# Merge gates of a hybrid decoder trunk: one 512-column product for both parts of the moving operand, and the halves of its bank added on the way out

## The chip, the cores and the metric

The kernel runs on one core of one Trainium2 chip. The metric is the device time of one execution in microseconds (us). TensorE is called PE, VectorE DVE, ScalarE ACT, GpSimd POOL, SyncE SP.

## The reference, cut to what matters

Two layers are computed for 256 tokens of width 1024, all in float32. In each layer one projection of the normalised tokens gives everything that the token mixers need, the two merge gates among it:

```python
h = rms_norm(x, norm_mix[l])
z = h @ w_in[l]
c_q, c_kv, k_pe, hq, hf, hi, hg, g_a, g_b = jnp.split(z, offsets, axis=-1)
y_a = mla_mixer(c_q, c_kv, k_pe, ...) @ w_proj_a[l]
y_b = hgrn2_mixer(hq, hf, hi, hg, ...) @ w_proj_b[l]
y = jax.nn.sigmoid(g_a) * y_a + jax.nn.sigmoid(g_b) * y_b
x = x + y @ w_out[l]
h = rms_norm(x, norm_ffn[l])
x = x + (jax.nn.silu(h @ w_gate[l]) * (h @ w_up[l])) @ w_down[l]
```

The gates g_a and g_b have 1024 columns each. They are the part of the projection that the change touches; the sigmoid is computed as a Tanh of half the value.

## The kernel before, in words

**Split operands.** PE takes float32 in a reduced form (F32R), so each operand is held as a high part and a low part, and a product a·b is computed as ah·bh + ah·bl + al·bh. A weight chunk of 2048 columns (two tiles of 8 blocks of 128 x 128) is loaded by one transfer into `st`; for each half of 1024 columns ACT casts the high part `wh` (line 115) and DVE subtracts to get the low part `wl` (line 117). There are three buffers for `st` and five for each of `wh` and `wl`; `weights` (line 122) lets the loads run one chunk ahead. The moving operand is `xx`, a tile in which for each k the high and the low part of the tokens lie side by side, 256 columns each.

**Two forms of a tile's product.** `mm3` (line 196) issues three products of 256 columns for each k (lines 206 to 208), all into the same 256 columns of a PSUM bank, so two tiles share one bank of 512 columns. `mmw` (line 210) multiplies the high weights by both parts at once, one product of 512 columns (line 214), and adds the low weights times the high part into the first half of the bank (line 215); the two halves of the bank are still to be added. The feed-forward stage has used `mmw` from the start: its gate and up tiles leave by an ACT copy of the second half (line 738), a DVE addition of the first (line 739) and a multiplication by the row scale `rb` (line 740, the first tile on DVE, the second on POOL). The down projection uses `mmw` too.

**The order of a layer.** `norm_in` makes `xx` and `rb`. Then come the chunks t0 to t2 and one chunk in token order, the latent projections of the attention, t3 to t6, and a hand-written interleaving (lines 679 to 691): before each of the chunks t7 to t16 one step of the generator `rec` (the recurrence) is issued, and before t8, t10, t12 and t14 one step of `at` (the attention). Chunks t9 to t16 hold the merge gates, sixteen tiles in a layer. After that come the projection `proj`, the output product `out`, a second `norm_in`, and the feed-forward stage. Within these lines a scheduler plans the order of each engine's instructions by a modelled timeline, with PSUM's and the buffers' slots in view; on the chip each engine then works through its instructions in that order.

**PSUM.** Four pools of two banks each: `acc`, `prj`, `trp`, `hgp`. A chunk of `tchunk` takes one bank of `acc` for its two tiles. `prj` serves the attention's scores, the last of which are issued before t12.

**A gate chunk's way out before.** `tchunk` (lines 267 to 287) multiplies the whole bank by `rb` on DVE into `gs` (line 286) and takes the Tanh on ACT into `gab` (line 287), which the projection stage uses at line 709.

Of the kernel before, what the change touches and what calls it, by code (L numbers as in the profile page):

```python
# [9 lines left out]
F32 = mybir.dt.float32  # L10
# [3 lines left out]
AF = mybir.ActivationFunctionType  # L14
ALU = mybir.AluOpType
AX = mybir.AxisListType

P = 128
T = 256
TT = T // P  # L20
D = 1024
KD = D // P
# [59 lines left out]
def trunk(ctx: ExitStack, tc: tile.TileContext, x_in, w_in, vec_in, gqk_in, cst_in, msk_in, out):  # L82
    nc = tc.nc
    V, S, G, PE = nc.vector, nc.scalar, nc.gpsimd, nc.tensor
# [5 lines left out]
    wk = ctx.enter_context(tc.tile_pool(name="wk", bufs=2))  # L90
    acc = ctx.enter_context(tc.tile_pool(name="acc", bufs=2, space=bass.MemoryType.PSUM))
    prj = ctx.enter_context(tc.tile_pool(name="prj", bufs=2, space=bass.MemoryType.PSUM))
# [8 lines left out]
    def load(upto):  # L101
        while nxt[0] < min(upto, len(order)):
            l, n, w = order[nxt[0]]
            st = stage.tile([P, WMAX], F32, name="st")
            o = OFFS[n]
            step = w // 2 if nxt[0] == 1 else w
            for c in range(0, w, step):
                nc.sync.dma_start(st[:, c:c + step], w_in[l, :, o + c:o + c + step])
            sub = SUB[w]
            parts = []  # L110
            for c in range(0, w, sub):
                wh = wsp.tile([P, 1088], F32R, name="wh")
                wl = wsp.tile([P, 1088], F32R, name="wl")
                n_ = min(sub, w - c)
                S.copy(wh[:, :n_], st[:, c:c + n_])  # L115
                eng = G if (n, c // sub) in ON_POOL or nxt[0] == 0 else V
                eng.tensor_tensor(wl[:, :n_], st[:, c:c + n_], wh[:, :n_].bitcast(F32), ALU.subtract)  # L117
                parts.append((wh, wl))
            ready[(l, n)] = lambda o, m, parts=parts, sub=sub: tuple(t[:, o % sub:o % sub + m] for t in parts[o // sub])
            nxt[0] += 1  # L120

    def weights(l, n):
        i = order.index((l, n, dict(PLAN)[n]))
        load(i + 2)
        return ready.pop((l, n))
# [57 lines left out]
    def bc(ap, shape):  # L183
        return ap.broadcast_to(shape)
# [11 lines left out]
    def mm3(ps, pairs, late=False):  # L196
        n = len(pairs)
        if late:
            for i, ((ah, al), (bh, bl)) in enumerate(pairs):
                PE.matmul(ps, ah, bh, start=i == 0, stop=False)  # L200
                PE.matmul(ps, ah, bl, start=False, stop=False)
            for i, ((ah, al), (bh, bl)) in enumerate(pairs):
                PE.matmul(ps, al, bh, start=False, stop=i == n - 1)
            return
        for i, ((ah, al), (bh, bl)) in enumerate(pairs):
            PE.matmul(ps, ah, bh, start=i == 0, stop=False)  # L206
            PE.matmul(ps, ah, bl, start=False, stop=False)  # L207
            PE.matmul(ps, al, bh, start=False, stop=i == n - 1)  # L208

    def mmw(ps, items):  # L210

        n = len(items)
        for i, ((ah, al), b) in enumerate(items):
            PE.matmul(ps, ah, b, start=i == 0, stop=False)  # L214
            PE.matmul(ps[:, 0], al, b[:, 0], start=False, stop=i == n - 1)  # L215
# [19 lines left out]
    def norm_in(l, col):  # L235

        xx = lay.tile([P, KD, 2, T], F32R, name="xx")
        xh, xl = xx[:, :, 0], xx[:, :, 1]
        for k in range(KD):
            split(xh[:, k], xl[:, k], xT[:, k], vec[:, l, col + k:col + k + 1])  # L240
        ss = token_stats(xT, KD, both=True)
        ms = wk.tile([P, TT], F32, name="ms")
        V.tensor_scalar(ms, ss, 1.0 / D, EPS, ALU.mult, ALU.add)
        r = lay.tile([P, TT], F32, name="r")
        power(r, ms)
        dg = wk.tile([P, TT, P], F32, tag="gs", name="dg")
        for t in range(TT):
            V.tensor_scalar(dg[:, t], ident, r[:, t:t + 1], None, ALU.mult)
        ps = prj.tile([P, 512], F32, name="prj")
        PE.matmul(ps[:, :T], ones, dg.rearrange("p t c -> p (t c)"), start=True, stop=True)  # L250
        rb = lay.tile([P, T], F32, name="rb")
        S.copy(rb, ps[:, :T])
        return xx, xh, xl, r, rb

    for l in range(L):
        xx, xh, xl, r, rb = norm_in(l, V_MIX)
# [7 lines left out]
        sg = mixp.tile([P, HH, T], F32, name="sg")  # L264
        gab = mixp.tile([P, KD, 2, T], F32, name="gab")

        def tchunk(ci):
            W = weights(l, f"t{ci}")
            tiles = T_CHUNKS[ci]
            if ci == 2:  # L270
                ps = hgp.tile([P, 2, T], F32, name="hgp")
            else:
                ps = acc.tile([P, 2, T], F32, name="acc")
            for j in range(len(tiles)):
                o = j * KD * P
                mm3(ps[:, j], [(W(o + k * P, P), xs[k]) for k in range(KD)], late=l == 0 and ci == 0)
            n = len(tiles)
            a = tiles[0]
            rbb = bc(rb.unsqueeze(1), [P, n, T])
            for lo, hi, dst in ((0, 5, cq), (5, 9, hf), (9, 13, hq), (13, 17, sg)):  # L280
                if lo <= a < hi:
                    V.tensor_tensor(dst[:, a - lo:a - lo + n], ps[:, :n], rbb, ALU.mult)
            if a >= 17:
                m = (a - 17) // 2
                g = wk.tile([P, 2, T], F32, name="gs", bufs=2)
                V.tensor_tensor(g, ps, rbb, ALU.mult)
                S.activation(gab[:, m], g, AF.Tanh, scale=0.5)

        for ci in range(3):
            tchunk(ci)  # L290
# [23 lines left out]
        def hchunk(ci):  # L314
            n = 272
            W = weights(l, "hia" if ci == 0 else "hib")
            for t in range(TT):
                ps = (hgp.tile([P, 512], F32, name="hgp") if ci == 1 else acc.tile([P, 512], F32, name="acc"))
                tok = slice(t * P, (t + 1) * P)
                mm3(ps[:, :n], [((xh[:, k, tok], xl[:, k, tok]), W(k * n, n)) for k in range(KD)])  # L320
                nv = n if ci == 0 else 512 - n
# [46 lines left out]

        def keys(W, t, i):
            kr, mpe = kro[t]  # L370
            tok = slice(t * P, (t + 1) * P)
            ps = prj.tile([P, 512], F32, name="prj")
            mm3(ps, [((ch[:, 3 + k, tok], cl[:, 3 + k, tok]), W(k * 1024 + i * 512, 512)) for k in range(2)])
            pv = ps.rearrange("p (h d) -> p h d", d=NOPE + VD)
            hs = slice(4 * i, 4 * i + 4)
            s2 = wk.tile([P, 4, QK], F32, name="s2")
            kh = wk.tile([P, 4, QK], F32, tag="qk", bufs=4, name="kh")
            S.copy(kh[:, :, :NOPE], pv[:, :, :NOPE])
            S.copy(av[:, t, hs], pv[:, :, NOPE:])
            G.tensor_tensor(s2[:, :, :NOPE], kh[:, :, :NOPE], kh[:, :, :NOPE], ALU.mult)  # L380
            V.tensor_reduce(rks[t][:, i], s2[:, :, :NOPE], AX.X, ALU.add)
            return kh
# [16 lines left out]

        def queries(W, t, i):  # L400
            tok = slice(t * P, (t + 1) * P)
# [17 lines left out]
        W = weights(l, "ukv")  # L419
        for t in range(TT):  # L420
            later += key_scales(t, [keys(W, t, i) for i in range(2)])
        for i in range(2):
            W = weights(l, f"uq{i}")
# [246 lines left out]
        for ci in (3, 4):  # L670
            tchunk(ci)
            for h in (2 * ci - 6, 2 * ci - 5):
                gates(h)
            if ci == 4:
                next(at)
        tchunk(5)
        tchunk(6)
        next(at)
# [20 lines left out]
        for i in range(2):  # L699
# [6 lines left out]
            for c in range(4):  # L706
                m = 4 * i + c
                g = wk.tile([P, 2, T], F32, name="gs", bufs=2)
# [5 lines left out]
        for i in range(4):  # L714
            W = weights(l, f"out{i}")
            ps = acc.tile([P, 2, T], F32, name="acc")
# [8 lines left out]
        xx, xh, xl, r, rb = norm_in(l, V_FFN)  # L725
        ffp = tc.alloc_tile_pool(name=f"ffn{l}", bufs=1)
        ff2 = ffp.tile([P, KF, 2, T], F32R, name="ff2")
        for m in range(KF):
            W = weights(l, f"gu{m}")
# [4 lines left out]
            g = ffp.tile([P, 2, T], F32, name="g", bufs=2)  # L734
# [14 lines left out]
        for m in range(KD):  # L749
            ps = acc.tile([P, 2, T], F32, name="acc")  # L750
# [96 lines left out]
```

## Time and profile before

| what | value |
|---|---|
| median of 3 runs | 778.02 us (777.91 to 778.33) |
| the profiled execution | 778.14 us, span from first to last instruction 776.4 us |
| PE busy | 762.0 us, 98% of the span |
| DVE busy | 590.4 us, 76% |
| ACT busy | 430.3 us, 55% |
| POOL busy | 270.2 us, 35% |
| granted TensorE clock | 1.000 of full speed |

A row of the trace gives the start of an instruction or group, its duration, engine, line and operation, the output and input tiles by name with shape, and in brackets the idle time of the engine before it with what ended it. Products are pipelined: the duration of one includes time in which the next is already running, so PE's pace is read from the distance between starts.

### The profile page before, as it was taken

How to read it: one execution, taken by the hardware profiler on the slowest of the kernel's cores; microseconds unless marked ns; L12 is line 12 of the kernel's file. 1: busy time of each engine (PE TensorE's matmuls, PEld its weight loads, DVE VectorE, ACT ScalarE, POOL GpSimd, SP SyncE). 2: the span in 40 equal slices, each digit the busy share in tenths (PEclk: the TensorE clock that was granted, in tenths of full speed). 3: DMA queues.
4: the chain of work that ended last, by engine and by line, in shares of the span. 5: the costliest groups of instructions: out<-in, count | busy, mean ns of one | idle time of the engine just before them, and what ended most of it. 6: DMA issues, size and time to landing. Idle time of an engine off the chain costs nothing.

```text
span 776.4 us, 14295 instructions
## 1 busy us (share of the span) xinstructions
PE 762.0 (98%) x5664; PEld 707.8 (91%) x5664; DVE 590.4 (76%) x876; ACT 430.3 (55%) x780; POOL 270.2 (35%) x283
## 2 busy tenths in 40 slices
PE   5999999999999999999999999999999999999998
PEld 4999999999988888888899999999999888888886
DVE  7789876568979888886657987756787988888552
ACT  5668755444655555554447786545355646565430
POOL 5585422014333444421035823211332353434000
PEclk9999999999999999999999999999999999999999
DMA  6754344336655556566544544343464555555730
GB/s 226 269 171 164 122 152 158 114 112 214 206 175 173 207 170 210 169 211 195 186 145 163 172 158 164 109 164 124 151 216 161 184 199 198 181 189 192 237 123 20
DMA packets 20658, 133.07 MB, mean 171 GB/s; under 512 B 2416, under 2 KB 3696, under 8 KB 5360
## 3 DMA queue, kind: packets, MB, share of 16 engines
q1 hardware_dynamic: 20592, 132.17, 50.5%
q8 instruction: 44, 0.72, 0.4%
q14 instruction: 22, 0.18, 0.1%
HBM read 131.11 MB, written 1.05 MB: 170 GB/s over the span
## 4 chain that ended last, share of the span: by engine, by line
PE 88%; DVE 5%; POOL 3%; issue 2%; ACT 1%; DMA 1%; SPq 0%; POOLq 0%; DVEq 0%; ACTq 0%
PE acc L214 16%; PE acc L206 10%; PE acc L207 10%; PE acc L208 10%; PE acc L215 8%; PE trp L214 5%; PE hgp L214 5%; PE prj L214 5%; PE trp L215 3%; PE hgp L215 3%; PE prj L215 3%; DVE wl L117 2%; PE prj L450 1%; PE trp L472 1%; POOL sq L229 1%
## 5 line engine op out<-in xcount | busy, mean ns | idle before, releaser
L117 DVE TENSOR_TENSOR wl<-st,wh 128x1024 fp32r<-128x1024 f32 (+3 forms) x241 | 325.7, 1354 | 71.8 <-ACT wh L115 71.2
L115 ACT CAST wh<-st 128x1024 fp32r<-128x1024 f32 (+2 forms) x250 | 257.5, 1034 | 155.0 <-PE acc L207 58.8
L206 PE MATMUL acc<-xx,wh 128*128 128x256 f32 x488 | 140.1, 287 | 0.0
L208 PE MATMUL acc<-xx,wl 128*128 128x256 f32 x488 | 139.0, 286 | 0.2 <-DVE wl L117 0.2
L207 PE MATMUL acc<-xx,wh 128*128 128x256 f32 x488 | 139.0, 285 | 0.0
L214 PE MATMUL acc<-ff,wh 128*128 128x512 f32 x352 | 123.3, 393 | 0.0
L215 PE MATMUL acc<-ff,wl 128*128 128x256 f32 x352 | 97.9, 279 | 0.0
L206 PEld LDWEIGHTS acc<-xx,wh 128*128 128x128 f32 x488 | 93.6, 192 | 0.7
L208 PEld LDWEIGHTS acc<-xx,wl 128*128 128x128 f32 x488 | 93.5, 192 | 0.4 <-DVE wl L117 0.4
L207 PEld LDWEIGHTS acc<-xx,wh 128*128 128x128 f32 x488 | 93.6, 192 | 0.0
L740 POOL TENSOR_TENSOR g<-g,rb 128x256 f32<-128x256 f32 x44 | 37.1, 844 | 135.4 <-DVE g L739 123.1
L214 PEld LDWEIGHTS acc<-ff,wh 128*128 128x128 f32 x352 | 66.0, 187 | 15.8
L193 ACT ACTIVATE ff<-hd 128x256 fp32r<-128x256 f32 x44 | 18.5, 419 | 94.3 <-POOL hd L745 94.3
L229 POOL TENSOR_TENSOR sq<-sq 128x256 f32<-128x256 f32 x34 | 34.1, 1004 | 100.1 <-ACT sq L223 62.2
L745 POOL TENSOR_TENSOR hd<-th,g 128x256 f32<-128x256 f32 x44 | 66.1, 1504 | 7.4 <-DVE th L743 4.5
L215 PEld LDWEIGHTS acc<-ff,wl 128*128 128x128 f32 x352 | 66.0, 187 | 0.1
L214 PE MATMUL prj<-xx,wh 128*128 128x512 f32 x176 | 62.4, 394 | 0.0
L214 PE MATMUL acc<-xx,wh 128*128 128x512 f32 x176 | 62.3, 393 | 0.0
L214 PE MATMUL hgp<-xx,wh 128*128 128x512 f32 x176 | 62.1, 392 | 0.0
L214 PE MATMUL trp<-xx,wh 128*128 128x512 f32 x176 | 62.1, 392 | 0.0
L215 PE MATMUL acc<-xx,wl 128*128 128x256 f32 x176 | 49.3, 280 | 0.0
L215 PE MATMUL trp<-xx,wl 128*128 128x256 f32 x176 | 49.0, 279 | 0.0
(240 smaller groups left out, 1720.2 us busy)
## 6 DMA issues: line engine op xcount, KB each, us to landing
st<-in_w_dram SPq DMA_DIRECT2D x115, 1024.0 KB, 4.8
st<-in_w_dram SPq DMA_DIRECT2D x4, 1088.0 KB, 4.9
st<-in_w_dram SPq DMA_DIRECT2D x4, 576.0 KB, 3.7
st<-in_w_dram SPq DMA_DIRECT2D x4, 512.0 KB, 5.4
xT<-in_x_dram SPq DMA_DIRECT2D x4, 256.0 KB, 5.8
out_dram<-xT SPq DMA_DIRECT2D x8, 128.0 KB, 1.9
cst<-in_cst_dram SPq DMA_DIRECT2D x1, 260.0 KB, 8.1
gqk<-in_gqk_dram SPq DMA_DIRECT2D x1, 192.0 KB, 9.2
```

The source lines that it names most:

```text
L115: S.copy(wh[:, :n_], st[:, c:c + n_])
L117: eng.tensor_tensor(wl[:, :n_], st[:, c:c + n_], wh[:, :n_].bitcast(F32), ALU.subtract)
L193: S.activation(hi, src, AF.Copy if isinstance(scale, float) else AF.Identity, scale=scale)
L206: PE.matmul(ps, ah, bh, start=i == 0, stop=False)
L207: PE.matmul(ps, ah, bl, start=False, stop=False)
L208: PE.matmul(ps, al, bh, start=False, stop=i == n - 1)
L214: PE.matmul(ps, ah, b, start=i == 0, stop=False)
L215: PE.matmul(ps[:, 0], al, b[:, 0], start=False, stop=i == n - 1)
L229: G.tensor_tensor(tot, tot, sq, ALU.add)
L450: PE.matmul(pv[:, h], qT[:, h0 + h, t * P:(t + 1) * P], kT[:, h0 + h, :ns], start=True, stop=True)
L740: (V, G)[j].tensor_tensor(g[:, j], g[:, j], rb, ALU.mult)
L745: G.tensor_tensor(hd, th, g[:, 1], ALU.mult)
```

## The change

Chunks t9 to t16 get a function of their own, `gchunk`. For each of the two tiles of a chunk it takes a whole bank, from `acc`, or for the second tile of t13 to t16 from `prj`, computes it with `mmw`, copies the second half out on ACT, adds the first on DVE, and multiplies by `rb` on DVE. One Tanh for both tiles stays. Weights, their loads and the interleaving stay as they are.

```diff
+        def gchunk(ci):
+
+            W = weights(l, f"t{ci}")
+            m = ci - 9
+            g = wk.tile([P, 2, T], F32, name="gs", bufs=2)
+            for j in range(2):
+                if ci > 12 and j:
+                    ps = prj.tile([P, 2, T], F32, name="prj")
+                else:
+                    ps = acc.tile([P, 2, T], F32, name="acc")
+                mmw(ps, [(W((j * KD + k) * P, P), xx[:, k]) for k in range(KD)])
+                S.copy(g[:, j], ps[:, 1])
+                V.tensor_tensor(g[:, j], g[:, j], ps[:, 0], ALU.add)
+                V.tensor_tensor(g[:, j], g[:, j], rb, ALU.mult)
+            S.activation(gab[:, m], g, AF.Tanh, scale=0.5)
+
         def tchunk(ci):
+            if ci > 8:
+                gchunk(ci)
+                return
...
-            if a >= 17:
-                m = (a - 17) // 2
-                g = wk.tile([P, 2, T], F32, name="gs", bufs=2)
-                V.tensor_tensor(g, ps, rbb, ALU.mult)
-                S.activation(gab[:, m], g, AF.Tanh, scale=0.5)
```

## Rows read from the trace of the kernel before

**Rows 1.** The page, busy time, share of the span and instructions of each engine.
```profile
PE 762.0 (98%) x5664; PEld 707.8 (91%) x5664; DVE 590.4 (76%) x876; ACT 430.3 (55%) x780; POOL 270.2 (35%) x283
```
**Rows 2.** Waits of PE: who waited for whom, us in total, times, longest.
```profile
PE acc L200 <- ACT xx L193: 7.0, 1, 7.0
...
PE acc L207 <- DVE yl L194: 0.4, 2, 0.2
PE acc L208 <- DVE wl L117: 0.2, 1, 0.2
```
**Rows 3.** Windows (length, busy PE, PEld, DVE, ACT, POOL; clock): layer 0's gates, feed-forward.
```profile
102.60:132.00 29.40, 29.40 (x379) 28.61 (x379) 21.32 (x35) 17.66 (x37) 7.78 (x11) 1.00 0.40 141
132.00:162.70 30.70, 30.70 (x268) 30.50 (x267) 18.75 (x24) 14.18 (x19) 3.56 (x3) 1.00 0.41 138
...
239.94:328.00 88.06, 88.06 (x510) 77.65 (x509) 74.08 (x113) 49.72 (x95) 38.14 (x32) 1.00 0.57 192
```
**Rows 4.** Timeline of PE in chunk t16, layer 0: line 206, eleven triples apart.
```profile
158.41 0.28 PE L206 MATMUL acc<-xx,wh 128*128 128x256 f32 x1
...
162.37 0.28 PE L206 MATMUL acc<-xx,wh 128*128 128x256 f32 x1
```
**Rows 5.** Timeline of PE, feed-forward: line 214, four pairs apart, then 32 pairs apart.
```profile
209.92 0.40 PE L214 MATMUL acc<-xx,wh 128*128 128x512 f32 x1
...
211.34 0.40 PE L214 MATMUL hgp<-xx,wh 128*128 128x512 f32 x1
...
265.78 0.39 PE L214 MATMUL acc<-xx,wh 128*128 128x512 f32 x1
...
276.87 0.39 PE L214 MATMUL acc<-xx,wh 128*128 128x512 f32 x1
```
**Rows 6.** Timeline of DVE, feed-forward: additions out of hgp, eight rounds of four tiles apart.
```profile
244.56 0.41 DVE L739 TENSOR_TENSOR g<-g,hgp 128x256 f32<-128x256 f32 x1
...
334.06 0.41 DVE L739 TENSOR_TENSOR g<-g,hgp 128x256 f32<-128x256 f32 x1
```
**Rows 7.** Single lines (min/median/max ns), and two groups of the page (busy us, mean ns).
```profile
L286 DVE TENSOR_TENSOR gs<-acc,rb x16: 676/688/692, 109.7 to 541.8; 128x512 f32<-128x512 f32 x16
L287 ACT ACTIVATE gab<-gs x16: 622/627/638, 110.4 to 542.6; 128x512 f32<-128x512 f32 x16
L738 ACT COPY g<-acc x22: 354/367/375, 217.8 to 704.9; 128x256 f32<-128x256 f32 x22
L739 DVE TENSOR_TENSOR g<-g,acc x22: 406/407/414, 219.0 to 707.0; 128x256 f32<-128x256 f32 x22
L740 DVE TENSOR_TENSOR g<-g,rb x44: 410/419/423, 225.2 to 714.0; 128x256 f32<-128x256 f32 x44
L117 DVE TENSOR_TENSOR wl<-st,wh 128x1024 fp32r<-128x1024 f32 (+3 forms) x241 | 325.7, 1354 | 71.8 <-ACT wh L115 71.2
L115 ACT CAST wh<-st 128x1024 fp32r<-128x1024 f32 (+2 forms) x250 | 257.5, 1034 | 155.0 <-PE acc L207 58.8
```
**Rows 8.** Groups of DVE in 102.6 to 132 us: busy, mean ns, idle before.
```profile
L117 DVE TENSOR_TENSOR wl<-st,wh 128x1024 fp32r<-128x1024 f32 x8 | 9.8, 1221 | 4.5 <-ACT wh L115 4.5
...
L527 DVE TENSOR_TENSOR hq<-hq,tot 128x512 f32<-128x512 f32 x2 | 1.7, 839 | 0.0
...
L453 DVE TENSOR_REDUCE mx<-prj 128x2 f32<-128x512 f32 x2 | 1.4, 683 | 0.0
...
L527 DVE TENSOR_TENSOR hq<-hq,ff 128x512 f32<-128x512 f32 x1 | 0.7, 694 | 0.8 <-POOL rows L638 0.8
...
L474 DVE RECIPROCAL rs<-sm 128x2 f32<-128x2 f32 x2 | 0.3, 165 | 2.5 <-ACT pr L460 2.5
```
**Rows 9.** Timeline of ACT, layer 0: a cast before t15's way out.
```profile
152.00 1.05 ACT L115 CAST wh<-st 128x1024 fp32r<-128x1024 f32 x1 [1.69 <-PE acc L207]
```
**Rows 10.** Timelines of DVE and PE where layer 0's gate stage ends.
```profile
167.45 0.69 DVE L194 SCALAR_TENSOR_TENSOR bl<-ob,bh 128x512 fp32r<-128x512 f32 x1 [0.70 <-ACT bh L193]
...
169.41 0.28 PE L207 MATMUL acc<-bl,wh 128*128 128x256 f32 x1
```

## The prediction

> **What bounds the kernel now.** I read the page first, then the waits, then the same stretches at three scales (windows, timeline, single lines). The page gives the shares: PE is busy 98% of a 776.4 us span, DVE 76%, ACT 55% [rows 1]. Busy time alone proves little, because pipelined products overlap in it, so the waits of PE decide: after the start of the program, where layer 0's first normalisation holds it up, PE waits for other engines in three more times only, 0.6 us together [rows 2]. So whatever PE work is taken away shortens the run, as long as DVE and ACT still deliver. The windows say how near these are: in the stretch that holds the merge gates of layer 0, PE is busy all the time, DVE 21.3 of 29.4 us (73%) in the first half and 18.8 of 30.7 us (61%) in the second; in the feed-forward stage, which already uses the new form, DVE is busy 74.1 of 88.1 us (84%) with PE still full [rows 3].
>
> **The product, the part removed.** A gate tile takes, for each of 8 values of k, three products of 256 columns. Their price is the distance between starts, not the duration that a row shows (280 ns, which overlaps with the next). Between the two starts in [rows 4] lie eleven triples: 3.96/11 = 360 ns each, 120 ns a product. The new form is one product of 512 columns and one of 256, with the weights loaded twice in place of three times. The feed-forward stage has it with the same moving tile: between the two starts of [rows 5] that are farthest apart as tiles go (265.78 and 276.87) lie four tiles, 32 pairs: 11.09/32 = 346.6 ns. That is 13.4 ns less than a triple. It is not the only pace: at the head of the same stage four pairs take 1.42 us, 355 ns [rows 5], and the evictions of that stage come every 89.50/8 = 11.19 us per four tiles, 349.7 ns a pair, since DVE there slips slowly behind PE [rows 6].
> There are 16 gate tiles in a layer, two layers, 8 pairs in a tile: 256 pairs. The gain on PE is 256 x 13.4 ns = 3.4 us at the steady pace, 256 x 10.3 ns = 2.6 us at the pace of the evictions, 256 x 5 ns = 1.3 us at that of the head. I take 3.4 us, because the triples that go have the most regular spacing of all and the steady pair is the same operation on the same kind of tile, and keep 1.3 us for the range.
> A rule speaks against most of this. The rows say that a product costs about 120 ns for 256 columns, and 347 - 120 = 227 ns for 512, so one product fewer is worth 13 ns. The Trainium skill, TensorE: Matmul & The Clock Gate, section "Back-to-back issue gap", gives a warm product its columns over 2.4 GHz plus a fixed 2.5 ns; by that a triple is 327.5 ns, a pair 325.0 ns, and the whole change is worth an estimated 0.6 us. The trace does not agree with that fixed part.
>
> **The way out, the part added.** Before, a chunk (two tiles in one bank) left by one DVE multiplication, 688 ns, and one Tanh on ACT, 627 ns. Now each tile has a bank of its own and leaves by an ACT copy (367 ns as in the feed-forward stage), a DVE addition (407 ns) and a DVE multiplication (419 ns); the Tanh stays [rows 7]. ACT gets 2 x 367 = 0.73 us more for a chunk; DVE 2 x (407 + 419) - 688 = 0.96 us more, 15.4 us over 16 chunks. None of it is on PE's path if the engines have room. The room: about four chunks fall in each half of the stretch, so DVE would be busy 21.3 + 3.9 = 25.2 of about 28.6 us (29.4 less half of a layer's 1.7 us), 88%, in the first half and 22.6 of 29.9 us (76%) in the second [rows 3]. The second is below what the feed-forward stage bears, the first above it. ACT, at 17.7 of 29.4 us there, goes to some 72%. The cover is thus DVE's idle time, and in the first half part of that is not free: DVE waits 4.5 us for casts of weights, 2.5 us for exponentials, 0.8 us for POOL [rows 8].
> **The banks.** The chunks t9 to t12 take both tiles from the pool acc, which has two banks; from t13 on the second tile of a chunk comes from prj, so four banks turn. With four banks a tile may leave three tiles later, 8 us; no stall. With two, a tile must be out while the next one is computed: 8 x 347 = 2.8 us, plus whatever attention and recurrence products PE does between. On free engines the way out takes 367 + 407 = 0.8 us; behind a cast of weights on ACT (1.03 us) and a subtraction on DVE (1.35 us) [rows 7] 3.2 us. So a turn costs between nothing and 0.4 us with one obstacle on each engine. A gain is excluded: before, PE never waited here. For eight such tiles in a layer, sixteen in all: 0 to 6 us. I take 0.7 us, nearer the lower end, since only a tile that meets both obstacles stalls and since between some tiles PE does attention and recurrence products.
> **Weights.** Casts in the second half wait for PE itself to free a buffer [rows 9], so weights are held up by PE and not the other way; a stage faster by 3% leaves them 0.1 us less per tile. DMA traffic is unchanged. I cost both at nothing; the cover is that wait of 1.7 us before a cast, and if it went, weights would be late by what is missing.
> **The end of the stage.** What is late next is the recurrence's last product: its low part starts on DVE at 167.45 and takes 0.69 us, PE uses it at 169.41 [rows 10], 1.27 us of slack. PE's own work before it that gets shorter is one tile or so, 0.1 us, and DVE gets up to 0.96 us more in that time. It just fits; between nothing and 0.3 us, I take nothing. Projection, output and feed-forward follow from PE's arrival and shift as a whole.
>
> **Sum.** 3.4 us less 0.7 us: 2.7 us. The profiled execution took 778.14 us (span 776.4 us), 0.12 us over the median of the runs, 778.02; from the median this gives 775.3 us, 0.35% faster. A difference of 0.2%, 1.56 us, is about what a measurement of this kernel can tell from no change.
>
> **Rivals.**
> First, the gain is eaten: pairs run at 350 to 355 ns in this stage, as they do in places of the feed-forward stage, and stalls at the two banks take another microsecond: 778.0 - 1.3 to 2.6 + 1.0 to 2.0, about 777.3 us. For it speaks DVE at 88% in the first half; against it that PE does not wait anywhere in the feed-forward stage at 84%. 25%.
> Second, the product saved was nearly free: if 512 columns cost twice what 256 do, 240 ns, a pair is 360 ns and nothing is gained: 778.0 us. The row at 346.6 ns speaks against it. 4%. By the 2.5 ns of the Trainium skill (the section above) the time would be an estimated 777.4 us.
> Third, slower: DVE becomes the bound in t9 to t12. Additions sit in order behind two DVE instructions, a subtraction of 1.35 us and a recurrence or attention step of 0.68 to 0.84 us, as DVE's queue there is a mixture of these [rows 8]. With the copy behind a cast the way out is 367 + 1030 + 1350 + 700 + 407 = 3.85 us against 2.8 us: 1.05 us a turn. At all sixteen turns 16.8 us (791 us), at half of them 8.4 us: 778.0 - 3.4 + 8.4 = 783.0 us. It decides from five such turns on (5.25 us against 3.4 + 1.56 us). Against it: waits of such length are nowhere on PE today, and the instruction order is planned with PSUM's banks in view. 13%.
> That the change doesn't do what it says can hardly be: one instruction fewer in each triple will be seen at once.
>
> **How the numbers follow.** Forecast 775.3 us, 58%: its own range is 774.5 (the steady pace, nothing lost) to 776.4 us. The first two rivals, 29%, are no measurable change; the third, 13%, is slower. The range for 8 in 10 starts at 774.5 us and reaches through most of the first two rivals to 778.8 us, leaving the third out. Faster 0.58, same 0.29, slower 0.13.
>
> **What would show it.** Right: gate tiles appear under lines of the form of 214 and 215, with starts 347 ns apart; PE's waits stay under some 1.5 us, and the gate stretch of each layer is 1.2 to 1.7 us shorter; DVE's busy time rises by some 15 us and ACT's by 12 us. Wrong in size: pairs at 353 ns or more. Wrong in kind: rows of PE waiting for the new addition, together over 3 us, or DVE idle no more in the first half of the stretch while PE waits; or a later stage that takes back what the gate stretch gave.

## The result and the profile after

The changed kernel takes 783.36 us (783.23 to 783.68) against 778.17 us before in the same runs: ratio 1.0068, interval 1.0054 to 1.0082. It is 5.2 us slower, where 2.7 us less was forecast. The profiled span grew from 776.4 to 781.5 us.

The page after, span and busy time by engine; it answers to [rows 1]:

```profile
span 781.5 us, 13860 instructions
...
PE 761.9 (97%) x5408; PEld 692.7 (89%) x5408; DVE 605.1 (77%) x924; ACT 438.9 (56%) x812; POOL 270.2 (35%) x283
```

The added work is close to what was worked out on DVE, 14.7 us more (15.4 forecast), and smaller on ACT, 8.6 us more (12 forecast). PE's busy time is the same, which says nothing, since overlapping products are counted as one stretch. The waits of PE say more; they answer to [rows 2]:

```profile
PE acc L200 <- ACT xx L193: 6.7, 1, 6.7
PE acc L206 <- ACT bh L193: 3.0, 2, 1.5
PE acc L201 <- DVE xx L194: 2.6, 1, 2.6
PE trp L232 <- POOL sq L229: 1.5, 2, 0.8
PE acc L214 <- DVE gs L279: 1.5, 2, 0.7
```

Two rows are new, and each stands twice, once in a layer: 1.5 us for `bh`, the recurrence's output, where the projection takes it over, and 0.7 us for `gs`, the addition on a gate tile's way out. The row of POOL counts one wait more, 0.8 us at 20.2 us of layer 0; it lies far ahead of the change, and the stretches below begin at the same time with it and without it (86.99 and 86.97 us).

Where the time went is read from the starts of four products in each trace. The table gives, for layer 0, the gate stretch (from the second round of recurrence products, at 86.97 us in the kernel before, to the first projection product, which reads `ah`), the hand-over (from there to the first product that reads `bh`), and the rest of the projection (to the first product that reads `yh`). Layer 1 repeats the differences within 0.1 us except where the text says otherwise. The runs are explained in the next section. They come from four sets, in each of which the kernel before ran too, with medians from 778.02 to 778.28 us; the ratios below are to the kernel before of the same set.

| kernel | time, us | gate stretch | hand-over | rest of projection | the three together |
|---|---|---|---|---|---|
| before | 778.2 | 75.76 | 6.20 | 17.28 | 99.24 |
| after | 783.36 | 76.35 | 7.87 | 17.62 | 101.84 |
| e1, new form in t9 to t12 | 780.71 | 76.92 | 6.18 | 17.28 | 100.38 |
| e2, new form in t13 to t16 | 782.08 | 75.34 | 7.86 | 19.11 | 102.31 |
| e3, three products, new way out | 780.86 | 77.15 | 6.20 | 17.28 | 100.63 |
| e4, one multiplication on POOL | 782.62 | 75.89 | 7.86 | 17.62 | 101.37 |
| e5, after with PE's order mended | 780.65 | 76.35 | 6.80 | 17.28 | 100.43 |
| e6, before with that order spoilt | 783.62 | 75.75 | 7.86 | 19.12 | 102.73 |
| e7, after with priority | 779.86 | 77.00 | 4.31 | 18.72 | 100.03 |
| e8 and e12, t13 to t16 with priority | 777.51, 777.38 | 75.78 | 4.32 | 18.72 | 98.82 |
| e9, e7 with four banks throughout | 777.07 | 75.67 | 4.33 | 18.72 | 98.72 |
| e10, e8 with two banks | 779.52 | 72.79 | 4.57 | 21.36 | 98.72 |
| e11, before with priority | 780.75 | 76.19 | 5.76 | 17.28 | 99.23 |

So the change costs 2.6 us a layer by the time the output product begins: 0.6 us in the gate stretch, which was to become 1.2 to 1.7 us shorter, 1.67 us in the hand-over and 0.34 us behind it. In e7 to e12 the plan mixes the products of neighbouring stretches (in e10 the first projection products stand ahead of the last gate products, and with priority the recurrence's last transposes stand in the gate stretch), so against the kernel before only the sum of the three compares.

**The product.** The timeline of PE in the new form, layer 0: starts of line 214, 14 pairs apart in t9, then 25 pairs apart in t15 and t16:

```profile
103.89 0.39 PE L214 MATMUL acc<-xx,wh 128*128 128x512 f32 x1
...
108.82 0.40 PE L214 MATMUL acc<-xx,wh 128*128 128x512 f32 x1
...
150.37 0.40 PE L214 MATMUL acc<-xx,wh 128*128 128x512 f32 x1
...
159.04 0.39 PE L214 MATMUL prj<-xx,wh 128*128 128x512 f32 x1
```

The first give 4.93/14 = 352 ns a pair, the second 8.67/25 = 347 ns, against 360 ns for the triple of [rows 4]. Both paces of [rows 5] occur, mostly the slower one up to some 148 us.

**The way out at two banks.** Timeline of ACT, DVE and PE at the head of t11, the first row of PE's wait for `gs`:

```profile
117.90 1.04 ACT L115 CAST wh<-st 128x1024 fp32r<-128x1024 f32 x1
...
118.84 0.38 ACT L278 COPY gs<-acc 128x256 f32<-128x256 f32 x1
118.98 1.23 DVE L117 TENSOR_TENSOR wl<-st,wh 128x1024 fp32r<-128x1024 f32 x1 [0.77 <-ACT wh L115]
...
120.12 0.41 DVE L279 TENSOR_TENSOR gs<-gs,acc 128x256 f32<-128x256 f32 x1
...
120.59 0.50 PE L214 MATMUL acc<-xx,wh 128*128 128x512 f32 x1 [0.74 <-DVE gs L279]
```

The tile in question was finished at about 115.7 us. Its copy stood behind four exponentials of the attention and a cast and began at 118.84; its addition stood behind a subtraction, which itself waited for that cast. The tile was out at 120.5, 4.8 us after its last product, and the next product in PE's order was the one that needs its bank.

**The hand-over.** Timelines of DVE, PE and ACT in layer 0 after, where the gate stage ends; they answer to [rows 10]:

```profile
163.34 0.28 PE L206 MATMUL acc<-ah,wh 128*128 128x256 f32 x1
...
165.98 0.69 DVE L615 TENSOR_TENSOR ono<-hgp,ro 128x512 f32<-128x512 f32 x1
...
169.10 0.60 PE L618 MATMUL hgp<-cst,ono 128*128 128x128 f32 x4
169.74 0.75 DVE L620 SCALAR_TENSOR_TENSOR ob<-hgp,vec,sg 128x512 f32<-128x512 f32 x1 [2.74 <-PE hgp L618]
170.53 0.63 ACT L193 ACTIVATE bh<-ob 128x512 fp32r<-128x512 f32 x1 [2.86 <-DVE ob L620]
...
171.21 0.51 PE L206 MATMUL acc<-bh,wh 128*128 128x256 f32 x2 [1.50 <-ACT bh L193]
```

`ono` is ready at 166.67, but the four transposes that read it begin at 169.10. PE is not waiting in between: it works through projection products of `ah` that stand ahead of the transposes in its order. Only when all 48 are done does it transpose, and then it has nothing to do until `ob` and `bh` are through. DVE and ACT stand still for 2.7 and 2.9 us in the meantime. Before the change, 22 of these 48 products stood ahead of the transposes; the same places before:

```profile
162.20 0.68 DVE L601 TENSOR_TENSOR ono<-hgp,ro 128x512 f32<-128x512 f32 x1
...
162.73 0.28 PE L206 MATMUL acc<-ah,wh 128*128 128x256 f32 x1
...
165.36 0.60 PE L604 MATMUL hgp<-cst,ono 128*128 128x128 f32 x4
...
168.93 0.40 PE L206 MATMUL acc<-bh,wh 128*128 128x256 f32 x2
```

`ono` itself comes later too: 3.3 us after the first projection product, where before it was 0.2 us (162.88 against 162.73). But before, it then lay ready for 2.5 us, so most of this delay had room.

### The profile page after: what moved, and what is told of

It reads as the page before. It is cut to its first block, busy times and chain, and to the rows that moved or that the text cites. A ratio compares the mean times of both kernels' runs of the same rounds, so it can differ in the third digit from the quotient of the medians.

```text
span 781.5 us, 13860 instructions
## 1 busy us (share of the span) xinstructions
PE 761.9 (97%) x5408; PEld 692.7 (89%) x5408; DVE 605.1 (77%) x924; ACT 438.9 (56%) x812; POOL 270.2 (35%) x283
## 4 chain that ended last, share of the span: by engine, by line
PE 83%; DVE 8%; POOL 3%; issue 3%; ACT 2%; DMA 1%; SPq 0%; POOLq 0%; DVEq 0%
PE acc L214 20%; PE acc L215 10%; PE prj L214 7%; PE acc L207 6%; PE acc L206 6%; PE acc L208 5%; PE hgp L214 5%; PE trp L214 5%; PE prj L215 4%; DVE wl L117 3%; PE hgp L215 3%; PE trp L215 3%; POOL sq L229 1%; PE trp L486 1%; PE prj L206 1%
## 5 line engine op out<-in xcount | busy, mean ns | idle before, releaser
L214 PE MATMUL acc<-xx,wh 128*128 128x512 f32 x368 | 132.4, 399 | 1.5 <-DVE gs L279 1.5
L215 PE MATMUL acc<-xx,wl 128*128 128x256 f32 x368 | 103.2, 280 | 0.0
L214 PE MATMUL prj<-xx,wh 128*128 128x512 f32 x240 | 85.5, 395 | 0.0
L214 PEld LDWEIGHTS acc<-xx,wh 128*128 128x128 f32 x368 | 69.0, 188 | 17.7 <-DVE gs L279 2.0
L215 PEld LDWEIGHTS acc<-xx,wl 128*128 128x128 f32 x368 | 69.4, 189 | 0.0
L215 PE MATMUL prj<-xx,wl 128*128 128x256 f32 x240 | 67.1, 280 | 0.0
L207 PE MATMUL acc<-xx,wh 128*128 128x256 f32 x232 | 66.3, 287 | 0.0
L208 PE MATMUL acc<-xx,wl 128*128 128x256 f32 x232 | 66.0, 286 | 0.2 <-DVE wl L117 0.2
L206 PE MATMUL acc<-xx,wh 128*128 128x256 f32 x232 | 66.0, 285 | 0.0
L214 PEld LDWEIGHTS prj<-xx,wh 128*128 128x128 f32 x240 | 45.0, 187 | 10.0
```

## The experiments

The theories, as far as they were formed after the result: **A**, DVE's added work in t13 to t16 delays the recurrence; **B**, the loss arises at the two banks in t9 to t12; **C** (formed after e3), the hand-over loses by PE's order; **D** and **E** on the early half: the two banks, or ACT and DVE being full. Every version is planned anew, so a difference between two runs can hold other changes of order besides the one that was meant.

**e1 and e2: the new form in half of the chunks.** `tchunk` calls `gchunk` only for these chunks, the others keep the old lines.

```diff
-            if ci > 8:
+            if 8 < ci < 13:
```

Expected of e1: 

> New form in t9 to t12 only, old form in t13 to t16. Theory A (the loss of 5.2 us is mainly at the end of the gate stage: DVE's added work in t13 to t16 delays the recurrence's last steps, and PE waits for their product at the hand-over to the projection): the hand-over is as before, the stall of 0.7 us a layer at t11 and the added interruptions stay, about 779.5 us (779 to 780.5). Theory B (the loss comes from the two banks and DVE's load in t9 to t12): nearly all of the loss stays, 782 to 783.5 us.

e2 has `if ci > 12:` in the same place. Expected of e2: 

> New form in t13 to t16 only, old form in t9 to t12. Theory A: the hand-over stays late, PE's wait for bh of some 1.5 us a layer stays, 781 to 783 us. Theory B: no loss, the gain of half the pairs, 776 to 777 us.

Measured: e1 780.71 us, 1.0034 (1.0020 to 1.0048); e2 782.08 us, 1.0048 (1.0030 to 1.0066). The halves lose different things, so neither A nor B is the whole: e1 lies just above A's range and below B's, e2 within A's. The early half lengthens the gate stretch by 1.16 us a layer and leaves the hand-over alone; the late half shortens the gate stretch by 0.42 us and brings the late hand-over.

**e3: the product split again, the way out kept.**

```diff
-                mmw(ps, [(W((j * KD + k) * P, P), xx[:, k]) for k in range(KD)])
+                for k in range(KD):
+                    ah, al = W((j * KD + k) * P, P)
+                    PE.matmul(ps[:, 0], ah, xx[:, k, 0], start=k == 0, stop=False)
+                    PE.matmul(ps[:, 1], ah, xx[:, k, 1], start=False, stop=False)
+                    PE.matmul(ps[:, 0], al, xx[:, k, 0], start=False, stop=k == KD - 1)
```

> The way out of the new kernel kept, the product of 512 columns split again into two of 256 (high weights times high part into the first half, times low part into the second). If the new product gives in this stage what its starts show (353 ns for the first half, 347 ns for the second, against 360 ns), the time rises above the new kernel by 256 x 10 ns = 2.6 us, to about 786 us (785 to 786.5). If the product gains nothing on the path here (the chain of DVE sets the end of the stage): 783 to 784 us.

Measured: 780.86 us, 1.0038 (1.0024 to 1.0051). A miss on both sides: with the slower product the kernel is 2.5 us faster than with the new one. The table shows why. The gate stretch is 0.80 us a layer longer, so the new product does save, 0.80/128 = 6.3 ns a pair. (PE's wait for the addition is 0.2 us a layer shorter in e3, 1.1 against 1.5 us in both layers, so the product by itself saves 1.0 us, 8 ns a pair.) But the hand-over is as before, 6.20 us, and PE's wait for `bh` is gone, although DVE and ACT do the same work on the way out as in the changed kernel. That spoke against theory A and pointed at the order: in this kernel's trace PE's transposes stand after 29 of the 48 products, not after all.

```profile
164.29 0.28 PE L206 MATMUL acc<-ah,wh 128*128 128x256 f32 x1
...
167.77 0.60 PE L622 MATMUL hgp<-cst,ono 128*128 128x128 f32 x4
...
170.49 0.40 PE L206 MATMUL acc<-bh,wh 128*128 128x256 f32 x2
```

**e4: the second multiplication of a chunk on POOL.**

```diff
-                V.tensor_tensor(g[:, j], g[:, j], rb, ALU.mult)
+                (V, G)[j].tensor_tensor(g[:, j], g[:, j], rb, ALU.mult)
```

> Second multiplication of each chunk on POOL instead of DVE, as the feed-forward stage has it: 0.42 us less on DVE for a chunk. Theory A: the recurrence's last steps come earlier by some part of 4 x 0.42 us a layer, 780 to 782 us. Theory B: the additions in t9 to t12 come earlier too, so the stall of 0.7 us a layer at t11 goes, 781.5 us; the two are told apart by PE's wait for bh in the trace.

Measured: 782.62 us, 1.0063 (1.0047 to 1.0079), above both expectations. PE's wait for the addition falls from 1.5 to 0.5 us and the gate stretch by 0.46 us, but the hand-over is not moved at all. DVE's load is a part of the early loss and no part of the late one.

**e5 and e6: the order alone.** e5 mends it in the changed kernel: the products of the last two of the four projection tiles are issued after the last transpose (`last[0]`).

```diff
...
+                    with (tc.issue_after(last[0].ins) if i == s == 0 and c >= 2 else nullcontext()):
...
```

e6 spoils it in the kernel before: the generator of the recurrence stops ahead of its last transposes, and these and what follows are issued after the last of the 48 products (`lm`).

```diff
...
+                if i == s == 0:
+                    with tc.issue_after(lm.ins):
+                        for _ in rec:
+                            pass
...
```

Expected of e5: 

> The new kernel with one place in PE's order changed: the recurrence's last four transposes are issued after 24 of the 48 projection products that don't need them, not after all 48. Theory C (the hand-over loses its time by the order that the plan gave PE: the transposes' input is ready while PE still works through products put ahead of them): PE's wait for bh, 1.5 us a layer, shrinks to under 0.6 us and the stretch from the first ah product to the first bh product from 7.87 us to under 6.9 us; time 780 to 781.5 us. Theory A (DVE delays the recurrence itself): PE waits at the transposes instead, 782.5 to 783.5 us.

Expected of e6: 

> The kernel before, gates in the old form, with the recurrence's last four transposes put behind all 48 projection products that don't need them, as the new kernel has them. Theory C: the hand-over stretch grows from 6.2 to about 7.8 us in each layer, 3.3 to 4 us in all: 781.3 to 782 us. Theory A (it takes DVE's added work): no change, 778 to 778.5 us.

Measured: e5 780.65 us, 1.0035 (1.0022 to 1.0048); e6 783.62 us, 1.0071 (1.0056 to 1.0086). The waits of PE in e5, in which the row of `bh` is gone and one for `ono` has come:

```profile
PE acc L214 <- DVE gs L279: 1.5, 2, 0.7
PE trp L232 <- POOL sq L229: 1.0, 2, 0.7
PE hgp L620 <- DVE ono L617: 0.9, 2, 0.4
```

and in e6, the kernel before with nothing else changed:

```profile
PE acc L206 <- ACT bh L193: 3.0, 2, 1.5
```

Theory C is shown from both sides, and by the order alone: the gate stretch of e5 is that of the changed kernel, 76.35 us, and that of e6 is that of the kernel before, within 0.01 us. Mending the order takes (7.87 - 6.80) + (17.62 - 17.28) = 1.41 us a layer away, 2.8 of the 5.2 us. Putting the transposes where the changed kernel has them gives the kernel before the same 7.86 us hand-over and the same 1.5 us wait, without any of the new form, and with `ono` as early as before. Theory A keeps a small part: in e5 the hand-over is still 0.6 us longer than before, and PE waits 0.4 us a layer for `ono` behind 24 products. That e6 loses 2 us more than expected comes from the granted clock (last section).

**e7 and e8: the recurrence's output steps planned with priority**, e7 in the changed kernel, e8 with the new form in t13 to t16 alone.

```diff
-                rec_out(t)
+                with tc.high_priority():
+                    rec_out(t)
```

Expected of e7: 

> The new kernel with the recurrence's output steps given priority in the plan, so that they stand earlier in every engine's order. Theory C: no wait for bh is left, about 779.5 us (778.5 to 780.5): what remains is the gate stage, 0.6 us a layer longer than before. Theory A: the same DVE work in the same stage, so 782 us or more.

Expected of e8: 

> New form in t13 to t16 only, and the recurrence's output steps given priority in the plan. Theory C: no wait for bh, and the gate stage is 0.4 us a layer shorter than in the kernel before, as it was with the new form in these chunks alone: about 777.2 us (776.7 to 778), level with the kernel before or a little faster. Theory A: the hand-over stays late, 781 us or more.

Measured: e7 779.86 us, 1.0020 (1.0010 to 1.0030), as theory C has it; what is left is the early half, and PE's wait for the addition, 1.5 us, is still there. e8 777.51 us, 0.9992 (0.9982 to 1.0001), within the expected range, though the interval still holds 1.

**e9 and e10: the number of banks.** e9 is e7 with the second tile of t9 to t12 in a bank of `trp`; e10 is e8 with both tiles of t13 to t16 in `acc`.

```diff
-                if ci > 12 and j:
-                    ps = prj.tile([P, 2, T], F32, name="prj")
+                if j:
+                    ps = prj.tile([P, 2, T], F32, name="prj") if ci > 12 else trp.tile([P, 2, T], F32, name="trp")
```

Expected of e9: 

> The new kernel with priority for the recurrence's output steps, and in t9 to t12 the second tile of a chunk takes its bank from the attention's pool trp, so that four banks turn there too. Theory D (the early half loses 1.2 us a layer because a tile must leave its bank while the next one is computed): the stall of 0.7 us at t11 goes and the gate stage is 0.4 to 0.8 us a layer shorter than in the kernel before: 776.3 to 777.5 us. Theory E (it loses it because ACT and DVE are full there, and attention and recurrence steps come late whatever the banks): 779 to 780.5 us, PE's waits move to the attention's or the recurrence's products.

Expected of e10: 

> New form in t13 to t16 alone with priority, but both tiles of a chunk from the two banks of acc, prj left out. Theory D: these chunks now lose as the early ones do, 0.7 us or more of PE waits for the addition in each layer, 779 us or more. Theory E: with ACT and DVE less full in this half two banks suffice, 777.3 to 778 us.

Measured: e9 777.07 us, 0.9988 (0.9979 to 0.9998), the lowest time of the study, though only 0.3 us below e12 of the same set. PE's waits, in which neither new row is left:

```profile
PE acc L200 <- ACT xx L193: 6.5, 1, 6.5
PE acc L201 <- DVE xx L194: 2.6, 1, 2.6
PE trp L232 <- POOL sq L229: 0.7, 1, 0.7
PE acc L207 <- DVE yl L194: 0.5, 2, 0.2
PE acc L208 <- DVE wl L117: 0.2, 1, 0.2
```

Its gate stretch is 1.33 us a layer shorter than that of e7, so theory D holds for the early half. Against the kernel before it is only 0.09 us shorter, where 0.4 to 0.8 us was expected; the three stretches together are 0.52 us shorter. DVE is even busier there than in the changed kernel; windows of the early half, length and busy time of PE, PEld, DVE, ACT, POOL, first after, then e9:

```profile
102.60:132.90 30.30, 29.56 (x318) 25.18 (x317) 24.47 (x44) 19.57 (x45) 7.61 (x11) 1.00 0.39 136
```

```profile
102.60:132.90 30.30, 30.30 (x322) 26.21 (x315) 24.92 (x46) 19.31 (x44) 8.09 (x11) 1.00 0.38 136
```

With two more banks PE is busy all the time with DVE at 82%: DVE was not the bound. e10, 779.52 us, 1.0018 (1.0009 to 1.0027), is slower than e8 as theory D said, but not for its reason: PE never waits for the addition, and the three stretches together are as short as in e9, 98.72 us. What it loses, it loses in the output product, where PE now waits 1.1 us a layer for the low part of the last projection tile:

```profile
PE acc L207 <- DVE yl L194: 2.1, 2, 1.1
```

So two banks suffice where ACT and DVE are less full, as theory E had it, and the new plan has put another wait elsewhere.

**e11 and e12: control and repetition.** e11 has the edit of e7 in the kernel before; e12 is e8 again.

Expected of e11: 

> The kernel before, with priority for the recurrence's output steps and nothing else: the control for the run with the new form in t13 to t16 and this priority. PE waits nowhere in this stretch before, so an earlier recurrence can give it nothing: 778.0 to 778.4 us. If the priority alone gives 0.5 us or more, the gain of that run is not the new form's.

Expected of e12: 

> The version with the new form in t13 to t16 and priority for the recurrence's output steps, again with more rounds, on the chip of its control: 128 of the 256 pairs save some 6.5 ns each, 0.8 us: 777.2 to 777.6 us, a ratio of 0.999 to the kernel before.

Measured: e11 780.75 us, 1.0036 (1.0023 to 1.0049); e12 777.38 us, 0.9990 (0.9981 to 0.9999). The control missed its value on the slow side: until the output product it is level with the kernel before (99.23 us), and then it has the same 1.1 us wait a layer for `yl` as e10. The priority alone thus gives nothing, and the 0.7 us that e12 gains agrees with 2 x 0.42 us of shorter stretches.

## Why the prediction was wrong, point by point

**The direction.** The sum was -3.4 + 0.7 + 0 us. The same three terms, with what the runs give: the product -2 x 0.80 = -1.6 us (e3 against after); other work within the gate stretch +2 x 1.40 = +2.8 us (0.60 net and 0.80 for the product); the end of the stage +2 x 2.01 = +4.0 us. Together +5.2 us. The first two alone are +1.2 us, so the sign would have been wrong without the third as well; e7, in which the hand-over is mended, is 1.6 us slower than the kernel before.

**The step that failed** is "The end of the stage": "It just fits; between nothing and 0.3 us, I take nothing." It measured 4.0 us. The step compared the time at which DVE delivers `bl` with the time at which PE uses it [rows 10], with PE's order taken as given. But that order is no constant of the kernel. It is planned anew for every version, and in the new plan the last transposes stood behind 26 more products. The front of this document says that a scheduler plans the order; the prediction drew on that once, as an argument against a rival, and left it out of its own sum. DVE's added work is not what moves the hand-over: e3 has the same work without the loss, e4 less of it with the whole loss, and e6 none of it with the loss. The step's bound of 0.96 us for DVE was too small all the same: `ono` comes 3.2 us later against PE's first projection product, of which 2.5 us was room that the step did not count.

**The product** was mis-sized. The steady pace was taken (13.4 ns a pair), the effect in place is 6.3 ns (8 ns without the longer wait at the banks), between the bounds of 5 and 13.4 ns. The head of the feed-forward stage [rows 5] was the nearer row: about half of the gate pairs ran at 352 ns. By the 2.5 ns of the Trainium skill (TensorE: Matmul & The Clock Gate, "Back-to-back issue gap") it would have been an estimated 0.6 us in all; the runs show 6.3 ns a pair in place of 2.5.

**The banks** were right in mechanism and too cheap: 0.7 us was taken of a range of 0 to 6, and 2.8 us stands in its place. The early half costs 1.16 us a layer by itself (e1), with its product's gain in it. The price was made of one obstacle on each engine, 3.2 us; at t11 the copy had four exponentials and a cast ahead of it, and the way out took 4.8 us. Of the 1.4 us a layer (e3 against the kernel before) the profile names 0.55 us as a wait, 0.74 us in the changed kernel; the rest lies in the distances between starts where PE changes between gate products and others and among those others, and no row names it.

**The rivals.** The third had the sign and nearly the time, 783.0 us, but by luck, since its cause was DVE as the bound at eight turns. There is one turn a layer with a wait, and e9 is fastest with DVE busier than in the changed kernel. The first was nearly right within the gate stretch: a product worth 1.3 to 2.6 us (1.6 measured) and stalls of 1.0 to 2.0 us (1.5 us of named waits); it lacked the rest of the interruptions and the hand-over. The second, pairs at 360 ns, didn't happen.

**A slip in the reading.** [Rows 2] leave out a row of 0.7 us for POOL at line 232, which the sentence "0.6 us together" passes over. Nothing hung on it.

**What stays open** is why the plan put the transposes so late. The recurrence as a whole moved back in it: PE's transposes for the first half of the tokens begin 4.1 us ahead of the first projection product, against 6.7 us before. The plan is made before the chip is reached; that it counts the 512-column product cheaper than the chip does is a guess that no run tried. Likewise open is why the priority creates the wait for `yl` in e10 and e11 and not in e8.

## What to carry to other kernels

When a scheduler plans each engine's order, a change in one stage also draws new orders for its neighbours: look in the trace for an operand that is ready while its reader stands behind work that doesn't need it, and fix that order by hand before judging the change. A cheaper product that needs a bank per tile halves the time a tile has to leave; price the way out with the longest row of the queue ahead of it, not with one obstacle, and give it more banks. With order and banks mended the change is worth about 0.1% here (e9, whose interval ends at 0.9998).

## What the runs showed of the hardware

A short wait of PE can be followed by a lower clock and then costs more than its length. In e6 PE is idle for 1.5 us of the 3 us from 168 to 171, and in the next windows the granted clock falls (the third number from the end); then the same windows of the changed kernel, with 1.5 us of idle time over the two and no fall:

```profile
168.00:171.00 3.00, 1.50 (x13) 1.26 (x12) 1.05 (x2) 0.63 (x1) 0.00 (x0) 1.00 0.00 0
171.00:174.00 3.00, 3.00 (x16) 2.81 (x16) 0.40 (x1) 0.11 (x1) 0.00 (x0) 0.61 0.00 0
174.00:177.00 3.00, 3.00 (x24) 3.00 (x23) 2.72 (x3) 2.14 (x3) 0.74 (x1) 0.82 0.00 0
```

```profile
168.00:171.00 3.00, 1.70 (x15) 1.46 (x13) 0.75 (x1) 0.47 (x1) 0.00 (x0) 1.00 0.00 0
171.00:174.00 3.00, 2.79 (x21) 2.60 (x22) 1.14 (x2) 0.72 (x2) 0.00 (x0) 1.00 0.00 0
```

A mean of 0.61 says that PE ran at the lower of its two levels, 1.2 of 2.4 GHz, for most of that window. The price is the rest of the projection, 19.12 us in both layers of e6 against 17.62 us after the same wait without the fall: 1.5 us. In e2 it happened in layer 0 only (19.11 and 17.62 us). It does not happen in every execution, as the mean granted clocks of the executions show: in e6 0.995 at 785.02 us, 0.997 at 783.86 and 783.39 us, 0.999 at 782.35 us; in e2 0.998 at 782.86 and 782.56 us, 0.999 and 1.000 at 781.05 and 781.60 us; in e4 0.997 for one execution of 784.03 us, 0.999 or more for the other three, up to 782.82 us. The execution of e6 at 0.999 is 4.1 us above the kernel before of its set; with 17.62 us for the rest of the projection, as after the same wait without the fall, the table gives 4.0 us. All four executions of the changed kernel are at 1.000. What decides whether the clock falls is not known.

The pair of products has two steady paces, 352 and 347 ns, in stretches of ten microseconds and more at full granted clock, while the triple of the gate chunks keeps 360 ns. They do not go with the chunk: in e8 the pairs of t13 to t16 run mostly at the slower pace, where those of t15 and t16 in the changed kernel run at the faster. What sets them was not tried.
